# RMSNorm with a swish on one core: every load and store of x on one queue, in one fixed order

## The chip, the core and the metric

The kernel runs on one core of a Trainium2 chip. The core has engines that work side by side: VectorE (DVE in the profile), ScalarE (ACT), GpSimd (POOL) and SyncE (SP), which computes nothing here and only issues transfers. TensorE is not used. Data lives in HBM (called dram in the code) and is worked on in the on-chip memory SBUF, which has 128 partitions. Transfers between the two (DMAs) are carried by 16 DMA engines, which all queues share. An instruction on SyncE or ScalarE *issues* a transfer: it puts it into that engine's queue and goes on; the data moves later, and a semaphore is raised when all of it has landed. In the profile SyncE's queue is q1 and ScalarE's is q10.

The metric is the device time of one execution in microseconds, the median of several.

## What is computed

`x` is 16 x 1024 x 512 float32, that is 16384 rows of 512 numbers. Each row is divided by its root mean square, multiplied by `gamma`, and put through x * sigmoid(x):

```python
rms = np.sqrt(np.mean(x ** 2, axis=-1, keepdims=True) + eps)
x_norm = x / rms * gamma
return x_norm * (1.0 / (1.0 + np.exp(-x_norm)))
```

So 33.55 MB are read and 33.55 MB are written.

## The kernel before, in words

**Tiling.** The 16384 rows are cut into 8 groups of 2048. In a group each of the 128 partitions has 16 consecutive rows, so over all groups a partition has 128 rows of 2 KB. In this document "a row" is one such row in every partition, 128 x 2 KB = 262144 bytes. The buffer `xb` (line 65) holds 96 rows per partition and is worked on in place: loaded, normed, swished, stored. Groups 6 and 7 take the places of groups 0 and 1 (`slots`, line 29).

**Compute.** The work goes in 32 chunks of `cn` = 4 rows. For a chunk ScalarE squares two rows with a running sum (line 164) and two rows into PSUM (line 171), VectorE sums the latter (line 217), GpSimd makes the inverse root (lines 145 and 152), VectorE multiplies each row by it and by gamma (line 228), and ScalarE applies Silu (line 183), which raises the semaphore `s_swish`. On ScalarE the Silu of a chunk follows the squares of the chunk two later, in an order written out by hand (the loop at line 206). Gamma is loaded once by ScalarE's queue (line 201) and spread over the partitions on VectorE (line 241). Just ahead of it ScalarE's queue carries a transfer of 8 KB from a zeroed tile `blank` to a DRAM tensor `scratch` (line 197), which nothing reads.

**Transfers of x.** A load or a store is a tuple of group, first row in the group, and number of rows. The 12 loads (lines 30 to 32) are issued by SyncE, in the list's order; the first two go out ahead of the start barrier (line 125). The first nine cover the 96 rows of the buffer and wait for nothing. Load 9, the 16 rows of group 6, is issued when stores 0 and 1 have landed (`over` and `behind`, lines 115 to 118); load 10 (12 rows) follows at once, and load 11 (4 rows) when store 2 has landed. The 10 stores (lines 33 to 35) are issued by ScalarE, on its own queue, between its computations. Store 0 is held until load 7 (the 12 rows up to row 92) has landed, and store 3 until load 10 has landed (`hold`, line 36, used at lines 186 to 191). The wait stands in ScalarE's own order of instructions, so what follows it on ScalarE, a Silu among it, waits too:

```python
    def store(t):
        if t in hold:
            nc.scalar.wait_ge(ld[hold[t][0]], 16)
```

With this the transfers go in four stretches: 96 rows of loads, 32 rows of stores, 32 rows of loads, 96 rows of stores. At each change of direction a transfer of 4 rows of the old direction (load 8, store 2, load 11) is still under way when the first of the new one is issued. At the end SyncE waits for the stores that it has not yet waited for (line 250).

Of the kernel before, what the change touches and what calls it, by code (L numbers as in the profile page):

```python
# [9 lines left out]
def kernel(  # L10
# [7 lines left out]
    nc = tc.nc  # L18
    P = nc.NUM_PARTITIONS
    AF = mybir.ActivationFunctionType  # L20
    ALU = mybir.AluOpType
    fp32 = mybir.dt.float32

    xf = x.flatten_outer_dims()
    of = out.flatten_outer_dims()
    R, D = xf.shape

    groups = [16] * 8
    slots = [0, 16, 32, 48, 64, 80, 0, 16]
    loads = [(0, 0, 4), (0, 4, 4), (0, 8, 8)]  # L30
    loads += [(g, 0, 16) for g in range(1, 5)]
    loads += [(5, 0, 12), (5, 12, 4), (6, 0, 16), (7, 0, 12), (7, 12, 4)]
    stores = [(0, 0, 16), (1, 0, 12), (1, 12, 4)]
    stores += [(g, 0, 16) for g in range(2, 7)]
    stores += [(7, 0, 8), (7, 8, 8)]
    hold = {0: (loads.index((5, 0, 12)), 12), 3: (loads.index((7, 0, 12)), 22)}
    behind = {loads.index((6, 0, 16)): 1}
    ring = 96
    early = 2
    cn = 4  # L40
    n_sq = 2

    first = [sum(groups[:g]) for g in range(len(groups))]
    assert P * sum(groups) == R, R
    assert all(s + n <= ring for s, n in zip(slots, groups))

    chunks = []
    for i, (g, r, n) in enumerate(loads):
        for c in range(r, r + n, cn):
            chunks.append((slots[g] + c, i if c == r else None))  # L50
    K = len(chunks)
    assert K * cn * P == R

    ends = [-(-(first[g] + r + n) // cn) for g, r, n in stores]

    inv_d = 1.0 / float(D)
    eps_f = float(eps)
# [4 lines left out]
    def sbuf(name, shape, dt=fp32):  # L62
        return nc.alloc_sbuf_tensor(name, shape, dt).ap()

    xb = sbuf("xb", [P, ring, D])
    gamma4 = sbuf("gamma4", [P, D])
    gamma_sb = sbuf("gamma_sb", [P, D])
    neg_half = sbuf("neg_half", [P, cn])
    ms = sbuf("ms", [P, K, cn])
    aeps = sbuf("aeps", [P, K, cn])  # L70
    rstd = sbuf("rstd", [P, K, cn])
    sq = [nc.alloc_psum_tensor(f"sq{i}", [P, n_sq, D], fp32).ap() for i in range(2)]
    junk = [nc.alloc_psum_tensor(f"junk{i}", [P, D], fp32).ap() for i in range(2)]

    ld = [nc.alloc_semaphore(f"ld{t}") for t in range(len(loads))]
    st = [nc.alloc_semaphore(f"st{t}") for t in range(len(stores))]
    scratch = nc.dram_tensor("scratch", [P, 16], fp32, kind="Internal").ap()
    blank = sbuf("blank", [P, 16])
    s_blank = nc.alloc_semaphore("s_blank")
    s_scratch = nc.alloc_semaphore("s_scratch")  # L80
    s_gld = nc.alloc_semaphore("s_gld")
    s_zero = nc.alloc_semaphore("s_zero")
    s_half = nc.alloc_semaphore("s_half")
# [7 lines left out]
    s_swish = nc.alloc_semaphore("s_swish")  # L91

    def need(ins, sem, value):
        return ins.wait_op(sem, value, "sem-ge")

    def dram(ap, piece):
        g, r, n = piece
        rows = ap[P * first[g] : P * (first[g] + groups[g])]
        return rows.rearrange("(p n) d -> p n d", n=groups[g])[:, r : r + n, :]

    def place(piece):
        g, r, n = piece
        return slots[g] + r, slots[g] + r + n

    def buf(piece):
        a, b = place(piece)
        return xb[:, a:b, :]

    stored_by_sync = set()

    def load(i):
        a, b = place(loads[i])
        for u, piece in enumerate(stores):
            c, d = place(piece)
            over = piece[0] < loads[i][0] and c < b and a < d
            if (over or behind.get(i) == u) and u not in stored_by_sync:
                nc.sync.wait_ge(st[u], 16)
                stored_by_sync.add(u)
        return nc.sync.dma_start(  # L119
            out=buf(loads[i]), in_=dram(xf, loads[i])  # L120
        ).then_inc(ld[i], 16)

    entry = nc.main_func.blocks[0].instructions
    here = nc.cur_bb.bb.instructions
    for t in range(early):
        ins = load(t).ins
        assert here[-1] is ins or here[-1].name == ins.name
        here.pop()
        at = next(
            i for i, other in enumerate(entry)  # L130
            if other.engine == mybir.EngineType.SP
            and isinstance(other, mybir.InstDrain)
        )
        entry.insert(at, ins)
    for t in range(early, len(loads)):
        load(t)
    nc.sync.wait_ge(s_scratch, 16)

    nc.gpsimd.memset(blank, 0.0).then_inc(s_blank, 1)  # L139
    nc.gpsimd.memset(gamma4, 0.0).then_inc(s_zero, 1)  # L140
    nc.gpsimd.memset(neg_half, -0.5).then_inc(s_half, 1)  # L141
    nc.gpsimd.wait_ge(s_half, 1)
    for k in range(K):
        need(
            nc.gpsimd.tensor_scalar(  # L145
                out=aeps[:, k, :], in0=ms[:, k, :], scalar1=eps_f, scalar2=None,
# [6 lines left out]
                out=rstd[:, k, :], in0=aeps[:, k, :], in1=neg_half, op=ALU.pow  # L153
# [2 lines left out]
        ).then_inc(s_rstd, 1)  # L156

    def square(k):
        at, landing = chunks[k]
        if landing is not None:  # L160
            nc.scalar.wait_ge(ld[landing], 16)  # L161
        for j in range(n_sq, cn):
            n = k * (cn - n_sq) + j - n_sq
            acc = nc.scalar.activation(  # L164
                out=junk[n % 2], in_=xb[:, at + j, :], func=AF.Square,
                scale=inv_d**0.5, accum_out=ms[:, k, j : j + 1],
            )
            if n >= 2:
                need(acc, s_acc, n - 1)
            acc.then_inc(s_acc, 1)  # L170
        square = nc.scalar.activation(  # L171
            out=sq[k % 2], in_=xb[:, at : at + n_sq, :],
            func=AF.Square, scale=inv_d**0.5,
        )
        if k >= 2:
            need(square, s_sum, k - 1)
        square.then_inc(s_sq, 1)

    def swish(k):
        at, _ = chunks[k]  # L180
        rows = xb[:, at : at + cn, :]
        need(
            nc.scalar.activation(out=rows, in_=rows, func=AF.Silu), s_norm, k + 1  # L183
        ).then_inc(s_swish, 1)

    def after(t):
        return max((k for u, (_, k) in hold.items() if u <= t), default=0)

    def store(t):
        if t in hold:  # L190
            nc.scalar.wait_ge(ld[hold[t][0]], 16)  # L191
        need(
            nc.scalar.dma_start(out=dram(of, stores[t]), in_=buf(stores[t])),  # L193
            s_swish, ends[t],
        ).then_inc(st[t], 16)

    need(nc.scalar.dma_start(out=scratch, in_=blank), s_blank, 1).then_inc(
        s_scratch, 16
    )
    need(  # L200
        nc.scalar.dma_start(out=gamma4[0:P:32, :], in_=gamma.partition_broadcast(4)),
        s_zero, 1,
    ).then_inc(s_gld, 16)
    nc.scalar.preload_act_table_set("silu_and_others")  # L204
    stored = 0
    for k in range(K + 3):
        if k < K:
            square(k)
        while stored < len(stores) and max(ends[stored] + 2, after(stored)) <= k:
            store(stored)  # L210
            stored += 1
        if 2 <= k < K + 2:
            swish(k - 2)

    def sums(k):
# [6 lines left out]
        ).then_inc(s_sum, 1)  # L222

    def norm(k):
        at, _ = chunks[k]
        for j in range(cn):
            row = xb[:, at + j, :]
            ins = nc.vector.scalar_tensor_tensor(  # L228
                out=row, in0=row, scalar=rstd[:, k, j : j + 1], in1=gamma_sb,
                op0=ALU.mult, op1=ALU.mult,  # L230
            )
            if j == 0:
                need(ins, s_rstd, k + 1)
        ins.then_inc(s_norm, 1)

    for k in range(K + 1):
        if k < K:
            sums(k)
        if k == 0:
            need(  # L240
                nc.vector.stream_shuffle(gamma_sb, gamma4, [0] * 32), s_gld, 16  # L241
            ).then_inc(s_gamma, 1)
        if k == 1:
            nc.vector.wait_ge(s_gamma, 1)
        if k >= 1:
            norm(k - 1)
# [39 lines left out]
```

## Time and profile before

| what | value |
|---|---|
| median of 3 runs | 160.73 us (160.39 to 161.25) |
| profiled execution, first to last instruction (span) | 159.0 us |
| bytes moved in the profiled execution | 67.16 MB, mean 422 GB/s |
| ScalarE busy | 129.6 us (82%) |
| VectorE busy | 124.4 us (78%) |
| GpSimd busy | 65.4 us (41%) |

The profile gives the profiled execution no other time than its span; the median of the runs is 1.73 us above it. Times inside the profile are counted from the span's start. Busy times are summed per engine. The DMA row of a page counts how many of the 16 DMA engines were carrying a packet; a packet is put down to the stretch that it starts in, so that a short stretch can show more than all 16 engines at work, and only stretches of several microseconds are to be compared.

### The profile page before, as it was taken

The numbers are of one execution on the slowest core, as the hardware profiler recorded it, in microseconds if no ns is written. First come the engines' busy times: TensorE is split into PE (matmuls) and PEld (weight loads), VectorE is DVE, ScalarE is ACT, GpSimd is POOL, SyncE is SP. The second block draws the span as 40 slices with busy tenths as digits, with TensorE's granted clock in tenths as the row PEclk, the third lists the DMA queues.
The fourth block names the chain that finished last, engine by engine and source line by source line (L and its number), as shares of the span: only waits on it lengthen the run. The fifth ranks groups of instructions, "written<-read, shape, count | busy, mean of one in ns | idle before, by whom it ended". The sixth has DMA issues, their size and how long they took to land.

```text
span 159.0 us, 507 instructions
## 1 busy us (share of the span) xinstructions
DVE 124.4 (78%) x162; ACT 129.6 (82%) x193; POOL 65.4 (41%) x71
## 2 busy tenths in 40 slices
DVE  0129999999999990299999999999999999994000
ACT  0946999999999913999999999999999999947000
POOL 2035555555555550055555555555555555550000
DMA  7999999999999999989899999999999999999997
GB/s 262 441 489 396 420 486 412 396 470 453 389 422 433 433 400 433 503 367 470 363 410 396 455 408 416 443 495 420 396 462 447 412 404 478 437 396 453 387 441 301
DMA packets 3324, 67.16 MB, mean 422 GB/s; under 512 B 500, under 2 KB 500, under 8 KB 504
## 3 DMA queue, kind: packets, MB, share of 16 engines
q1 hardware_dynamic: 1728, 33.56, 49.8%
q10 hardware_dynamic: 1592, 33.57, 49.2%
q14 instruction: 4, 0.03, 0.0%
HBM read 33.56 MB, written 33.56 MB: 422 GB/s over the span
## 4 chain that ended last, share of the span: by engine, by line
ACT 65%; DMA 12%; issue 5%; DVE 4%; ACTq 2%; another core or an unknown queue 2%; SPq 0%
ACT xb L183 27%; ACT junk L164 22%; ACT sq L171 16%; DMA xb<-in_x_dram 12%; DVE xb L228 3%; ACTq L193 2%; DVE ms L217 1%; SPq L119 0%; ACTq L191 0%; ACTq L161 0%
## 5 line engine op out<-in xcount | busy, mean ns | idle before, releaser
L228 DVE SCALAR_TENSOR_TENSOR xb<-xb,rstd,gamma_sb 128x512 f32<-128x512 f32 x128 | 87.2, 744 | 0.0
L183 ACT ACTIVATE xb<-xb 128x2048 f32<-128x2048 f32 x32 | 60.9, 1902 | 10.4 <-issue 6.3
L217 DVE TENSOR_REDUCE ms<-sq 128x2 f32<-128x1024 f32 x32 | 39.1, 1223 | 17.7 <-ACT sq L171 14.5
L145 POOL TENSOR_SCALAR aeps<-ms 128x4 f32<-128x4 f32 x32 | 20.6, 644 | 71.9 <-DVE ms L217 71.9
L152 POOL TENSOR_TENSOR rstd<-aeps,neg_half 128x4 f32<-128x4 f32 x32 | 44.0, 1376 | 2.7
L164 ACT ACTIVATE junk<-xb 128x512 f32<-128x512 f32 x64 | 37.2, 582 | 3.2 <-DMA xb<-in_x_dram 3.2
L171 ACT ACTIVATE sq<-xb 128x1024 f32<-128x1024 f32 x32 | 32.2, 1005 | 0.0
L164 ACT ACTIVATION_READ_ACCUMULATOR junk<-xb 128x1 f32 x64 | 11.9, 187 | 0.0
L204 ACT ACT_TABLE_LOAD x1 | 1.3, 1283 | 3.6 <-issue 3.6
L241 DVE LOAD_MASK_SELECT gamma_sb<-gamma x1 | 0.0, 14 | 2.8 <-DMA gamma<-in_gamma_dram 2.8
L139 POOL MEMSET blank<- 128x16 f32 x1 | 0.1, 112 | 1.5 <-POOLq L60 1.5
L241 DVE STREAM_SHUFFLE gamma_sb<-gamma 128x512 f32<-128x512 f32 x1 | 0.7, 717 | 0.0
L140 POOL MEMSET gamma<- 128x512 f32 x1 | 0.5, 524 | 0.0
L267 POOL MEMSET const-float32-0.0<- 128x1 f32 x1 | 0.1, 98 | 0.2 <-issue 0.2
L267 POOL MEMSET const-uint8-127<- 128x1 uint8 x1 | 0.1, 102 | 0.0
L267 POOL MEMSET const-bfloat16-1.0<- 128x1 bf16 x1 | 0.1, 101 | 0.0
L141 POOL MEMSET neg_half<- 128x4 f32 x1 | 0.1, 101 | 0.0
L267 POOL MEMSET const-float32-1.0<- 128x1 f32 x1 | 0.1, 98 | 0.0
## 6 DMA issues: line engine op xcount, KB each, us to landing
out_dram<-xb ACTq DMA_DIRECT2D x6, 4096.0 KB, 19.2
xb<-in_x_dram SPq DMA_DIRECT2D x5, 4096.0 KB, 28.8
xb<-in_x_dram SPq DMA_DIRECT2D x2, 3072.0 KB, 37.0
xb<-in_x_dram SPq DMA_DIRECT2D x4, 1024.0 KB, 13.3
out_dram<-xb ACTq DMA_DIRECT2D x2, 2048.0 KB, 13.0
out_dram<-xb ACTq DMA_DIRECT2D x1, 3072.0 KB, 19.0
xb<-in_x_dram SPq DMA_DIRECT2D x1, 2048.0 KB, 10.3
out_dram<-xb ACTq DMA_DIRECT2D x1, 1024.0 KB, 19.8
```

What stands on the lines that cost most here:

```text
L140: nc.gpsimd.memset(gamma4, 0.0).then_inc(s_zero, 1)
L145: nc.gpsimd.tensor_scalar(out=aeps[:, k, :], in0=ms[:, k, :], scalar1=eps_f, scalar2=None, op0=ALU.add,),
L152: nc.gpsimd.tensor_tensor(out=rstd[:, k, :], in0=aeps[:, k, :], in1=neg_half, op=ALU.pow),
L164: acc = nc.scalar.activation(out=junk[n % 2], in_=xb[:, at + j, :], func=AF.Square, scale=inv_d**0.5, accum_out=ms[:, k, j : j + 1],)
L171: square = nc.scalar.activation(out=sq[k % 2], in_=xb[:, at : at + n_sq, :], func=AF.Square, scale=inv_d**0.5,)
L183: nc.scalar.activation(out=rows, in_=rows, func=AF.Silu), s_norm, k + 1
L193: nc.scalar.dma_start(out=dram(of, stores[t]), in_=buf(stores[t])),
L204: nc.scalar.preload_act_table_set("silu_and_others")
L217: nc.vector.tensor_reduce(out=ms[:, k, 0:n_sq], in_=sq[k % 2], op=ALU.add, axis=mybir.AxisListType.X,),
L228: ins = nc.vector.scalar_tensor_tensor(out=row, in0=row, scalar=rstd[:, k, j : j + 1], in1=gamma_sb, op0=ALU.mult, op1=ALU.mult,)
L241: nc.vector.stream_shuffle(gamma_sb, gamma4, [0] * 32), s_gld, 16
L267: nc = _bacc.Bacc("TRN2", target_bir_lowering=False, num_devices=1)
```

## The change

All loads and all stores of x are issued by SyncE, on its one queue, in one order written out as a list: loads of rows 0 to 99, stores of rows 0 to 31 in pieces of 16, 8 and 8, loads of rows 100 to 127 in pieces of 12, 12 and 4, and then the stores of rows 32 to 127. A piece is now a first row (of the 128 of a partition) and a number of rows. The buffer is a ring of 100 rows per partition: row r lies at r modulo 100. A store carries its wait for `s_swish` on the issuing instruction; a load waits for the stores whose places it overwrites. The holds, the `behind` wait, the scratch transfer and its zeroed tile are gone, and ScalarE issues gamma alone. The chunks and the computation stay as they are.

```diff
-    slots = [0, 16, 32, 48, 64, 80, 0, 16]
-    loads = [(0, 0, 4), (0, 4, 4), (0, 8, 8)]
-    loads += [(g, 0, 16) for g in range(1, 5)]
-    loads += [(5, 0, 12), (5, 12, 4), (6, 0, 16), (7, 0, 12), (7, 12, 4)]
-    stores = [(0, 0, 16), (1, 0, 12), (1, 12, 4)]
-    stores += [(g, 0, 16) for g in range(2, 7)]
-    stores += [(7, 0, 8), (7, 8, 8)]
-    hold = {0: (loads.index((5, 0, 12)), 12), 3: (loads.index((7, 0, 12)), 22)}
-    behind = {loads.index((6, 0, 16)): 1}
-    ring = 96
+    ring = 100
+    loads = [(0, 4), (4, 4), (8, 8), (16, 16), (32, 16), (48, 16), (64, 16), (80, 16)]
+    loads += [(96, 4), (100, 12), (112, 12), (124, 4)]
+    stores = [(0, 16), (16, 8), (24, 8), (32, 16), (48, 16), (64, 16), (80, 16)]
+    stores += [(96, 4), (100, 12), (112, 8), (120, 8)]
+    order = [("load", i) for i in range(loads.index((100, 12)))]
+    order += [("store", t) for t in range(3)]
+    order += [("load", i) for i in range(loads.index((100, 12)), len(loads))]
+    order += [("store", t) for t in range(3, len(stores))]
...
     def load(i):
-        a, b = place(loads[i])
-        for u, piece in enumerate(stores):
-            c, d = place(piece)
-            over = piece[0] < loads[i][0] and c < b and a < d
-            if (over or behind.get(i) == u) and u not in stored_by_sync:
+        a, n = loads[i]
+        for u, (c, m) in enumerate(stores):
+            over = c + ring < a + n and a < c + m + ring
+            if over and u not in stored_by_sync:
                 nc.sync.wait_ge(st[u], 16)
                 stored_by_sync.add(u)
...
+    def store(t):
+        need(
+            nc.sync.dma_start(out=dram(of, stores[t]), in_=buf(stores[t])),
+            s_swish, ends[t],
+        ).then_inc(st[t], 16)
...
-    for t in range(early, len(loads)):
-        load(t)
-    nc.sync.wait_ge(s_scratch, 16)
-
-    nc.gpsimd.memset(blank, 0.0).then_inc(s_blank, 1)
+    for what, t in order[early:]:
+        load(t) if what == "load" else store(t)
+
...
     def square(k):
-        at, landing = chunks[k]
-        if landing is not None:
+        at = k * cn % ring
+        for landing in landings[k]:
             nc.scalar.wait_ge(ld[landing], 16)
...
-    def store(t):
-        if t in hold:
-            nc.scalar.wait_ge(ld[hold[t][0]], 16)
-        need(
-            nc.scalar.dma_start(out=dram(of, stores[t]), in_=buf(stores[t])),
-            s_swish, ends[t],
-        ).then_inc(st[t], 16)
-
-    need(nc.scalar.dma_start(out=scratch, in_=blank), s_blank, 1).then_inc(
-        s_scratch, 16
-    )
...
-    stored = 0
-    for k in range(K + 3):
+    for k in range(K + 2):
         if k < K:
             square(k)
-        while stored < len(stores) and max(ends[stored] + 2, after(stored)) <= k:
-            store(stored)
-            stored += 1
-        if 2 <= k < K + 2:
+        if k >= 2:
             swish(k - 2)
```

More of the change, by code (lines that the diff above doesn't have):

```diff
@@ L43 @@
     first = [sum(groups[:g]) for g in range(len(groups))]
[L44 to L54, printed above, removed]
+    rows_each = sum(groups)
+    assert P * rows_each == R, R
+    assert ring % cn == 0
+    for pieces in (loads, stores):
+        assert [a for a, _ in pieces] == [
+            sum(n for _, n in pieces[:i]) for i in range(len(pieces))
+        ]
+        assert sum(n for _, n in pieces) == rows_each
+    K = rows_each // cn
+    landings, seen = [], 0
+    for k in range(K):
+        landings.append([])
+        while seen < len(loads) and loads[seen][0] < (k + 1) * cn:
+            landings[k].append(seen)
+            seen += 1
+    ends = [-(-(a + n) // cn) for a, n in stores]
     inv_d = 1.0 / float(D)
@@ L76 @@
     st = [nc.alloc_semaphore(f"st{t}") for t in range(len(stores))]
[L77 to L80, printed above, removed]
     s_gld = nc.alloc_semaphore("s_gld")
@@ L96, in dram @@
     def dram(ap, piece):
-        g, r, n = piece
+        a, n = piece
+        g = max(g for g in range(len(groups)) if first[g] <= a)
+        r = a - first[g]
+        assert r + n <= groups[g], piece
         rows = ap[P * first[g] : P * (first[g] + groups[g])]
         return rows.rearrange("(p n) d -> p n d", n=groups[g])[:, r : r + n, :]
-    def place(piece):
-        g, r, n = piece
-        return slots[g] + r, slots[g] + r + n
     def buf(piece):
-        a, b = place(piece)
-        return xb[:, a:b, :]
+        a, n = piece
+        at = a % ring
+        assert at + n <= ring, piece
+        return xb[:, at : at + n, :]
     stored_by_sync = set()
     def load(i):
-        a, b = place(loads[i])
-        for u, piece in enumerate(stores):
-            c, d = place(piece)
-            over = piece[0] < loads[i][0] and c < b and a < d
-            if (over or behind.get(i) == u) and u not in stored_by_sync:
+        a, n = loads[i]
+        for u, (c, m) in enumerate(stores):
+            over = c + ring < a + n and a < c + m + ring
+            if over and u not in stored_by_sync:
                 nc.sync.wait_ge(st[u], 16)
@@ L179, in swish @@
     def swish(k):
-        at, _ = chunks[k]
+        at = k * cn % ring
         rows = xb[:, at : at + cn, :]
@@ L184, in swish @@
         ).then_inc(s_swish, 1)
-    def after(t):
-        return max((k for u, (_, k) in hold.items() if u <= t), default=0)
-    def store(t):
-        if t in hold:
-            nc.scalar.wait_ge(ld[hold[t][0]], 16)
-        need(
-            nc.scalar.dma_start(out=dram(of, stores[t]), in_=buf(stores[t])),
-            s_swish, ends[t],
-        ).then_inc(st[t], 16)
-    need(nc.scalar.dma_start(out=scratch, in_=blank), s_blank, 1).then_inc(
-        s_scratch, 16
-    )
     need(
@@ L224, in norm @@
     def norm(k):
-        at, _ = chunks[k]
+        at = k * cn % ring
         for j in range(cn):
```

## Prediction

> **What bounds the kernel now.** I read four things in this order: the page's top, the table of stretches, the waits of SyncE's queue, and the chain that ended last. From the page:
>
> ```profile
> span 159.0 us, 507 instructions
> ...
> DVE 124.4 (78%) x162; ACT 129.6 (82%) x193; POOL 65.4 (41%) x71
> ...
> DMA  7999999999999999989899999999999999999997
> ...
> q1 hardware_dynamic: 1728, 33.56, 49.8%
> q10 hardware_dynamic: 1592, 33.57, 49.2%
> ...
> ACT 65%; DMA 12%; issue 5%; DVE 4%; ACTq 2%; another core or an unknown queue 2%; SPq 0%
> ```
>
> No computing engine is above 82%. The packets of the two queues together take 49.8 + 49.2 = 99.0% of the time of the 16 DMA engines, and only the first and the last slice of the DMA row are visibly below nine tenths. The chain that ended last speaks against this with its "ACT 65%". It follows the last store back to the Silu that released it. But that store was issued at 146.82 and its 8 rows landed only at the end of the span, some 12 us later, although 8 rows need 8 x 0.605 = 4.8 us (262144 bytes at 433 GB/s are 0.605 us a row). It stood behind stores already queued. So the transfers bound the kernel, and what matters is where the flow is below its full rate. The table of stretches gives that (stretch in us; length; busy time of DVE, ACT and POOL; the clock of an engine not used here; DMA share; GB/s):
>
> ```profile
> 12.00:56.00 44.00, 42.29 (x55) 42.18 (x65) 22.49 (x22) 1.00 1.00 431
> 104.00:144.00 40.00, 38.89 (x52) 37.90 (x56) 20.14 (x20) 1.00 1.00 433
> 56.00:64.00 8.00, 3.89 (x6) 1.73 (x2) 2.04 (x2) 1.00 1.04 440
> 96.00:104.00 8.00, 7.76 (x11) 8.00 (x13) 4.11 (x5) 1.00 1.04 445
> 76.00:84.00 8.00, 7.76 (x11) 8.00 (x13) 4.11 (x5) 1.00 1.00 392
> 76.00:86.00 10.00, 9.76 (x14) 10.00 (x18) 5.91 (x6) 1.00 1.03 412
> 77.00:85.00 8.00, 7.76 (x12) 8.00 (x13) 4.11 (x5) 1.00 1.01 397
> ```
>
> Pure loads run at 431 GB/s, pure stores at 433. The two switches from loads to stores (near 60 and 100) lie in stretches of 440 and 445: nothing is lost there. The one switch from stores to loads (near 79) lies in 392 to 412. That is the only hole between start and end. The waits of SyncE's queue say why it is there:
>
> ```profile
> SPq L117 <- DMA out_dram<-xb: 73.0, 1, 73.0
> SPq L119 <- DMA out_dram<-xb: 1.0, 1, 1.0
> ```
>
> SyncE stood until 78.4 on the landing of store 1 (that is L117) and issued load 9 at 78.49. Of the stores only the 4 rows of store 2 were then left, 4 x 0.605 = 2.4 us at most; that store landed at 80.9, which is when the second wait ended. The stores ran out while the loads were only starting.
>
> **The change part by part.** The sum is made against the span of 159.0 us. The profile has no other time for this execution; the median, 160.73, is 1.73 us above it, and I let that stand unchanged.
>
> The floor first: 256 rows (128 in, 128 out) x 0.605 = 154.9 us, so 159.0 - 154.9 = 4.1 us are not flow. The stretch from 0 to 4 moves 260 GB/s, which costs (1 - 260/433) x 4 = 1.6 us. The same two loads go out ahead of the barrier in both kernels, so this stays. The change can touch the hole at 79 and the scratch transfer; the rest is start and tail, and the last store is 8 rows in both.
>
> The switch from stores to loads, removed: deficits of the three stretches against 433 are (1 - 392/433) x 8 = 0.76, (1 - 412/433) x 10 = 0.49, and (1 - 397/433) x 8 = 0.66 us. A packet counts in the stretch it starts in, and the 2 us from 84 to 86 that the longest stretch adds show 492 GB/s, more than the flow can carry: it borrows from later. So I take 0.76, and keep 0.49 as the other end.
>
> What is at that place in the new order? Load 9 (rows 100 to 111) waits for store 0 (16 rows) alone. When that has landed, stores 1 and 2, 16 rows or 9.7 us, are still queued on the same queue, against 2.4 us before. Load 10 waits for store 1 and has 8 + 12 rows ahead of it (12.1 us), load 11 waits for store 2 and has 24 rows ahead (14.5 us), and store 3 is issued right behind it. A landing is seen about a microsecond late and an issue takes 0.33 to 0.99 us (the line of the loads), so every one is queued long before its turn. What a switch inside one queue costs is shown by no row. From below: nothing, as in the stretches with the well-covered switches near 60 and 100 (a gain below nothing is excluded, the flow being at its full rate there). From above: 0.76, the switch near 79, which is the only one in this direction. I take nothing: with 9.7 us queued ahead, it is nearest to the switches whose successor was waiting.
>
> The two switches from loads to stores: near 60 and 100 they cost nothing with two queues. With one queue the stores of rows 0 to 31 need chunks 4, 6 and 8, whose Silus end at about 30, 38 and 46 (one every 3.99 us: L183 starts at 28.13, 32.12, 36.11), and their turn comes after 100 loads, at about 1.6 + 100 x 0.605 = 62. They are queued 16 us early. Bounds again 0 and 0.76 each; I take 0.
>
> The scratch transfer, removed: ScalarE's queue takes 1.8% of the DMA engines from 4 to 8 us and 1.2% from 8 to 12, together 0.12 us, gamma included. Gain 0.12, at least 0. Gamma is issued 0.45 us earlier (2.04 for 2.49); VectorE waited 2.8 us for it, but compute is not on the path.
>
> Stores leave ScalarE: the hold for load 7 kept the Silu of the eleventh chunk back by 6.28 us ("ACT xb L183 <- issue: 6.3"). Without it the last Silu ends near 146.8 - 6.3 = 140.5 instead of 146.8. Gain nothing, since the transfers hide it, and if that cover were gone it would be at most 6.3.
>
> Stores on SyncE wait for Silus, and behind such a wait stand all later issues of SyncE; nobody else waits on SyncE. Due times, by rows ahead in the order x 0.605 + 1.6: store 3 (160 rows ahead) 98, needs chunk 12, done near 62; the 12 rows from 100 (228 ahead) 139.5, chunk 28, near 126; the next 8 (240) 147, chunk 30, near 134; the last 8 (248) 152, chunk 32, near 141. The least slack is 11 us, so 0. The 11 issues added to SyncE at below 1 us each lie in the same slack. Loads for compute: row 100 is wanted by chunk 26 near 116 and lands near 90.
>
> The ring of 100: the 4 rows more are loaded before the first switch and fewer after it; the bytes are the same. Cost 0.
>
> Sum: -0.76 - 0.12 = -0.88. Span 158.1, median 160.73 - 0.88 = 159.85.
>
> **A rule beside the row.** The row is the hole near 79 and none near 60 and 100. The Trainium skill, "DMA: Bandwidth & Descriptors", section "Issuing engines are not separate DMA queues", speaks against any effect: transfers issued by different engines run on the same 16 DMA engines, and the choice of issuer only changes issue time. By that rule alone the hole would stay and the time would be 160.73. The same page, section "Two DMAs through the same engine are not ordered", says that inside one queue descriptors start in order but are pipelined; by that the hole goes and the time is that of my sum. The trace agrees with the first in the rates (431 and 433 GB/s on either queue) and says nothing on switches inside one queue.
>
> **The rivals.** A switch could cost the same wherever it is queued: the slow reads after 79 would then come from the turn itself, not from the late issue. For it: the first loads of the kernel also start slowly (260 GB/s up to 4 us). Against it: there too, nothing was queued ahead. Only the scratch transfer is saved then: 160.73 - 0.12 = 160.6. It is also the case of a change that does nothing.
>
> The slower one: with two queues a DMA engine that has finished its last load takes up a store from the other queue while other work is still in flight, and the switches near 60 and 100 are free because of that. In one queue each engine must go through the switch in order, and may stall at all three. At a price p each, the time changes by 3p - 0.88, so it is slower by over 0.80 from p = 0.56 up. At the price of the hole, 0.76, it is +1.40, or 162.1. At the price of the kernel's start, 1.6, it is +3.9, or 164.6. For it: no row shows a switch inside a queue, and the free ones all had two. Against it: within either queue one transfer follows another at 431 to 433 GB/s, with no step where one ends.
>
> Compute as the new bound is a third: the last store would have to be released later than about 152, and its chunk is due near 141. It would take 11 us of new delay, where 6.3 are removed; I give it no chance of its own.
>
> **How the numbers follow.** 0.5%, about what a measurement of this kernel can tell from no change, is 0.80 us; 159.93 is the line. Covered switches: 0.56, time 159.85, own range 159.4 to 160.3 (the hole at 0.49 gives 160.1; the runs of before spread over 0.9 us). Its middle is only just past the line, but the smaller reading of the hole is the weaker one, so 0.42 of it is faster and 0.14 the same. The switch that keeps its price: 0.14, same. Switches that cost in one queue: 0.30, slower. Together 0.42, 0.28, 0.30. The range runs from 159.4 to 162.2: it leaves out the dearer half of the slow rival, some 0.15.
>
> **What the profile after would show.** If I am right: a stretch of 8 us around the stores-to-loads switch, now near 82, at 425 GB/s or more; the same near 62 and 98; SyncE's queue with 99% of the packets' time, ScalarE's with gamma alone; the last Silu ending near 140; a span near 158.1. If the second case holds, a stretch near 82 stays below 412. If the third, the stretches near 62 and 98 fall below 420 as well. Silus ending after 150, or a load issued after the stores ahead of it have run out, would make the working wrong in its slack and not in its switches.

## The result, and the profile after

The changed kernel is slower: 161.42 us (161.28 to 161.94, 9 runs) against 160.53 us for the kernel before, a ratio of 1.0068 (95% interval 1.0054 to 1.0082). The forecast was 159.85. The time lies inside the range given, but on the other side of the kernel before than forecast. Of the runs below, three of the five executions of the kernel with late loads took 164.8 to 165.1 us, over 1.5% more than its fastest, and are left out of its ratio.

The page of the changed kernel, in the lines that answer to those shown of before:

```profile
span 160.6 us, 503 instructions
...
DVE 124.5 (78%) x162; ACT 129.6 (81%) x193; POOL 65.4 (41%) x70
...
DMA  7999999999999999999999999999999999899993
...
q1 hardware_dynamic: 3312, 67.11, 98.1%
q14 instruction: 4, 0.03, 0.0%
q10 hardware_dynamic: 8, 0.01, 0.0%
...
ACT 63%; DMA 12%; issue 7%; DVE 4%; SPq 0%; ACTq 0%
```

One queue now carries all of x. The dip near the middle of the DMA row is gone, but the last slice falls from 7 tenths to 3: something ends late. The table of stretches of the changed kernel (columns as before) looks at the three turns:

```profile
56.00:64.00 8.00, 7.74 (x10) 8.00 (x13) 4.09 (x4) 1.00 1.01 391
76.00:84.00 8.00, 7.74 (x10) 8.00 (x14) 4.09 (x4) 1.00 1.04 444
96.00:104.00 8.00, 7.74 (x10) 8.00 (x14) 4.09 (x4) 1.00 1.03 436
104.00:144.00 40.00, 33.62 (x44) 33.62 (x46) 16.36 (x16) 1.00 1.00 432
```

The hole near 79 is gone as forecast (444 for 392 GB/s). A new one of the same size is at the first turn, from loads to stores: 391 for 440 GB/s, which is (1 - 391/433) x 8 = 0.78 us. The last turn is free. So the holes of both kernels come to the same, and that does not make it slower. They are not alike, though, by the packets' own times in the trace. In the kernel before the first 32 KB load packets behind the turn are slow: between 79 and 80 they take 1.80 us (median), from 82 on 1.21. In the changed kernel the first 32 KB store packets take 1.21 at once, and the last loads ahead of the turn are slow: their 8 KB packets take 0.31 us up to 61 and 0.51 to 0.52 from 61 to 63 (medians).

The waits of SyncE's queue show no shortage either:

```profile
SPq L127 <- ACT xb L189: 93.2, 10, 24.7
SPq L121 <- DMA out_dram<-xb: 37.5, 3, 28.5
```

SyncE waits long, but ahead of time: the last store is issued at 140.4 and lands 20.1 us later, behind what was queued. The last Silu ends at 140.4, as worked out.

What is slower is the very end. The stretch from 158 to 160, first in the kernel before, then in the changed one:

```profile
158.00:160.00 2.00, 0.00 (x0) 0.00 (x0) 0.00 (x0) 1.00 0.02 8
```

```profile
158.00:160.00 2.00, 0.00 (x0) 0.00 (x0) 0.00 (x0) 1.00 0.08 33
```

One engine of 16 is a share of 0.06, and 433/16 = 27 GB/s. After 158 the changed kernel moves 33 GB/s: little more than one engine's work. The trace also has a 4-byte completion packet for each DMA on each of the 16 engines; their times show how far the last engine is behind the median one (us from the span's start, worked out from the trace's records):

```
completed, DMA                     before: median  last     after: median  last
load of rows 48 to 63                      40.62  41.05            40.56  40.82
load of rows 64 to 79                      50.33  51.23            50.30  51.14
last load before the first turn            60.11  61.01            63.36  64.85
last load of all                           99.88 100.28            99.81 102.06
last store                                158.11 158.63           157.99 160.24
```

The median engine ends 0.12 earlier in the changed kernel, which is the size of the scratch term. The last one is 2.25 us behind instead of 0.52 (the last but one is 1.1 behind). Together: -0.12 + 2.25 - 0.52 = +1.61, which is the last completion's move (158.63 to 160.24) and the growth of the span (159.0 to 160.6). The profiled execution was timed at 161.94, the highest of the nine; their spans go from 160.0 to 160.6, so the loss varies from run to run, and by the medians it is 0.89 and not 1.6.

The table also says when. Between 41 and 51 the last engine falls from 0.3 or 0.4 to 0.8 or 0.9 behind, in both kernels alike. In the changed kernel it is 1.5 behind at the end of the last load before the first turn, where the slow packets are, and 2.25 at the end of the last load of all. In the kernel before the lag goes from 0.8 at the end of store 2 to 0.4 at the end of load 9, over the hole near 79.

### The profile page after: what moved, and what is told of

It is laid out like the page before. It is cut to its first block, busy times and chain, and to the rows that moved or that the text cites. A ratio compares the mean times of both kernels' runs of the same rounds, so it can differ in the third digit from the quotient of the medians.

```text
span 160.6 us, 503 instructions
## 1 busy us (share of the span) xinstructions
DVE 124.5 (78%) x162; ACT 129.6 (81%) x193; POOL 65.4 (41%) x70
## 4 chain that ended last, share of the span: by engine, by line
ACT 63%; DMA 12%; issue 7%; DVE 4%; SPq 0%; ACTq 0%
ACT xb L189 25%; ACT junk L170 22%; ACT sq L177 16%; DMA xb<-in_x_dram 12%; DVE xb L216 3%; DVE ms L205 1%; SPq L121 0%; ACTq L167 0%
```

## The experiments

The runs shared runs of the kernel before, whose median was 160.3 to 160.5; ratios are to those.

**What makes the hole at the first turn?** Four kernels.

The scratch transfer put back on ScalarE's queue:

```diff
...
+    need(nc.scalar.dma_start(out=scratch, in_=blank), s_blank, 1).then_inc(
+        s_scratch, 16
+    )
     need(
         nc.scalar.dma_start(out=gamma4[0:P:32, :], in_=gamma.partition_broadcast(4)),
...
```

> The changed kernel with the scratch transfer of 8 KB back at the head of ScalarE's queue, SyncE's final wait for it included. The new hole (stretch 56 to 64 us at 391 GB/s in the changed kernel, 440 before) and 161.42 us against 160.53 are to be explained. Theory 'cold store': the first store of a run is slow, and the scratch transfer had paid for that at the start; then the stretch 56 to 64 is back at 425 or more and the time is near 160.6. Rival 'switch in one queue': loads followed by stores in one queue are slow wherever they stand; then the stretch stays near 391 and the time is 161.4 to 161.5.

Measured: 161.75 us (ratio 1.0095, 1.008 to 1.011), the stretch at 391. The time is some 0.3 above what the rival expected, but the theory of a cold store falls: the rate of the stretch did not come back.

The scratch transfer taken out of the kernel before:

```diff
...
-    nc.sync.wait_ge(s_scratch, 16)
...
-    need(nc.scalar.dma_start(out=scratch, in_=blank), s_blank, 1).then_inc(
-        s_scratch, 16
-    )
...
```

> The kernel before without the scratch transfer, its zeroed tile and the wait for it; nothing else moves. 'Cold store': the stretch 56 to 64 falls from 440 to about 391 and the time rises by about 0.9, to 161.4. 'Switch in one queue': the stretch stays near 440 and the time is that of the kernel before or 0.1 less, 160.4 to 160.5.

Measured: 160.42 us (1.0014, 0.9997 to 1.0031), the stretch at 440. No effect that can be told from none. My 0.12 for it is not visible in the time.

The first three stores issued from ScalarE again:

```diff
-    order += [("store", t) for t in range(3)]
...
+    def store(t, eng=nc.sync):
...
             square(k)
+        if k == 12:
+            nc.scalar.wait_ge(ld[loads.index((80, 16))], 16)
+            for t in range(3):
+                store(t, nc.scalar)
         if k >= 2:
             swish(k - 2)
```

> The changed kernel with its first three stores (rows 0 to 31) issued from ScalarE's queue, held there until the load of rows 80 to 95 has landed, as the kernel before does it; all else from SyncE, no scratch transfer. 'Switch in one queue': the stretch 56 to 64 is back at 425 or more and the time near 160.5. 'Cold store': nothing has warmed this queue either, the stretch stays near 391 and the time near 161.4.

Measured: 160.88 us (1.0044, 1.0025 to 1.0063), between the two expectations. The stretches near the first and the second turn:

```profile
56.00:64.00 8.00, 4.00 (x6) 0.24 (x1) 2.04 (x2) 1.00 1.06 451
...
76.00:84.00 8.00, 7.76 (x11) 8.00 (x13) 4.11 (x5) 1.00 1.01 369
```

The hole at the first turn is gone and one at the second is there, larger: here loads start on one queue while 16 rows of stores are still on the other, and both move side by side at 369 GB/s with the engines all busy (share 1.01). So crossing queues frees the first turn. That it is the two kinds in flight on two queues that make the second one dear is not shown: no other run has them.

A ring of 96, so that the first stretch ends with packets of 32 KB:

```diff
-    ring = 100
+    ring = 96
...
-    loads += [(96, 4), (100, 12), (112, 12), (124, 4)]
+    loads += [(96, 16), (112, 12), (124, 4)]
```

> The changed kernel with a ring of 96 rows: the first stretch of loads ends with the 16 rows from 80, in packets of 32 KB, not with the 4 rows from 96 in packets of 8 KB; the second is 16, 12 and 4 rows. 'Cold store' and 'switch in one queue' both expect the hole to stay, moved 2.4 us earlier, with about 392 GB/s in the stretch 54 to 62 and a time of 161.3 to 161.5. If it is the small packets ahead of the switch that are slow, the stretch is at 425 or more and the time near 160.6.

Measured: 162.19 us (1.011, 1.0092 to 1.0129), the stretch 54 to 62 at 360. The hole is larger and the time longer than expected (392; 161.3 to 161.5). The small packets are not the cause: here too the last loads ahead of the turn are the slow ones, with 32 KB packets of 1.49 to 2.03 us (medians from 57 to 60) for 1.21.

**Does every turn cost?** One more turn on the one queue:

```diff
-    order = [("load", i) for i in range(loads.index((100, 12)))]
-    order += [("store", t) for t in range(3)]
+    order = [("load", i) for i in range(loads.index((64, 16)))]
+    order += [("store", 0)]
+    order += [("load", i) for i in range(loads.index((64, 16)), loads.index((100, 12)))]
+    order += [("store", t) for t in range(1, 3)]
```

> The changed kernel with one more change of direction on its queue: after the loads of rows 0 to 63 comes the store of rows 0 to 15, then the loads of rows 64 to 99, then the stores of rows 16 to 31, and the rest as before. Loads now turn to stores near 40, 72 and 98 us, where they did near 62 and 98. The scratch transfer on ScalarE's queue did not help the changed kernel and its loss did not hurt the kernel before, so the first store of the core is not what is slow. Theory 'every switch': each turn from loads to stores in one queue costs what the first did, 0.9 us; then the stretches 36 to 44 and 68 to 76 both read about 391 GB/s and the time is 162.2 or more. Rival 'first of the queue': only the first store on a queue is slow; then 36 to 44 reads 391, 68 to 76 reads 425 or more, and the time stays at 161.4 to 161.6.

Measured: 161.74 us (1.0082, 1.0068 to 1.0095). The stretches at the first two turns from loads to stores:

```profile
36.00:44.00 8.00, 7.74 (x10) 8.00 (x14) 4.09 (x4) 1.00 0.94 337
...
68.00:76.00 8.00, 7.76 (x11) 8.00 (x13) 4.09 (x4) 1.00 0.99 408
```

The hole went to the first turn, at more than twice its size (1.77 us by the rate, where 391 would be 0.78), and the second, the same as the first turn of the changed kernel but for its place, lost 0.46. That is nearer to "the first of the queue", though 408 is short of the 425 expected. But the next kernel speaks against a simple form of that, a scratch transfer on SyncE's own queue:

```diff
...
+    need(nc.sync.dma_start(out=scratch, in_=blank), s_blank, 1).then_inc(
+        s_scratch, 16
+    )
     for what, t in order[early:]:
         load(t) if what == "load" else store(t)
...
```

> The changed kernel with the scratch transfer of 8 KB on SyncE's queue, behind the first two loads. 'First of the queue': this pays for the first store at the start, the stretch 56 to 64 is at 425 or more and the time near 160.6. 'Every switch': the stretch stays near 391 and the time is 161.4 to 161.7.

Measured: 162.0 us (1.0102, 1.0088 to 1.0115), the stretch 56 to 64 at 390. A store of 8 KB does not pay for it. The time is 0.3 above what "every switch" expected.

A kernel meant to have no hole, with the queues crossed at each turn from loads to stores:

```diff
-    order += [("store", t) for t in range(3)]
-    order += [("load", i) for i in range(loads.index((100, 12)), len(loads))]
...
+        if (what, t) == ("store", 3):
+            nc.sync.wait_ge(ld[loads.index((112, 12))], 16)
...
+        if k == 12:
+            nc.scalar.wait_ge(ld[loads.index((80, 16))], 16)
+            for t in range(3):
+                store(t, nc.scalar)
+        if k in (15, 17, 18):
+            load({15: 9, 17: 10, 18: 11}[k], nc.scalar)
```

> A kernel meant to have no hole: loads of rows 0 to 99 on SyncE's queue, the stores of rows 0 to 31 and behind them the loads of rows 100 to 127 on ScalarE's, the stores of rows 32 to 127 on SyncE's again, each first store held as in the kernel before until only 4 rows of loads are left. Every turn from loads to stores crosses queues, the turn from stores to loads stays inside one. No scratch transfer, ring of 100 rows. 'Switch in one queue' expects the stretches 56 to 64, 78 to 86 and 94 to 102 all at 425 or more; with holes adding up the time is near 159.7 (160.5 less 0.76), with a laggard setting the end near 160.2.

Measured: 160.69 us (1.0016, 1.0007 to 1.0025). The first turn is free and the hole is at the second, inside one queue and with its loads queued in time (the first was issued at 73.7, the stores ended at 83):

```profile
56.00:64.00 8.00, 3.87 (x5) 0.10 (x1) 2.04 (x2) 1.00 1.07 455
...
78.00:86.00 8.00, 7.76 (x11) 8.00 (x13) 4.11 (x5) 1.00 1.00 385
94.00:102.00 8.00, 7.76 (x11) 8.00 (x13) 4.11 (x5) 1.00 1.01 431
```

So a turn from stores to loads inside one queue is not free as such. The slow packets are again the last ones ahead of the turn: 16 KB packets of the stores take 1.21 us between 81 and 82, and 0.62 before. In all of these kernels at least one hole stands somewhere; what places it stays open.

**Does a hole cost the end?** The first loads of the second stretch issued late:

```diff
-    stores = [(0, 16), (16, 8), (24, 8), (32, 16), (48, 16), (64, 16), (80, 16)]
+    stores = [(0, 16), (16, 12), (28, 4), (32, 16), (48, 16), (64, 16), (80, 16)]
...
+            late = a == 100 and u == 1
+            if (over or late) and u not in stored_by_sync:
```

> The changed kernel with the first loads after the first stores issued late, as in the kernel before: the stores of rows 0 to 31 go as 16, 12 and 4 rows, and the load of rows 100 to 111 waits for the first two, so that only 4 rows are left ahead of it. The hole of about 0.75 us that the kernel before has at that place comes back (a stretch of 8 us near 80 at 390 to 400 GB/s). Theory 'holes add up': the time rises by 0.75, to 162.2. Rival 'laggard': in the changed kernel one of the 16 DMA engines ends 2.2 us after most of the others and sets the end, and a hole lets it catch up; then the time rises by less than 0.3, to 161.2 to 161.7, and the flow at the end stops more sharply (the stretch 156 to 161 above 164 GB/s).

Measured: ratio 1.0135 (1.0115 to 1.0155), from two executions of 162.22 and 162.88 us. The first turn keeps its hole (386 GB/s from 56 to 64). The expected hole came larger than in the kernel before and brought another at the third turn:

```profile
78.00:86.00 8.00, 7.76 (x11) 8.00 (x13) 4.11 (x5) 1.00 0.89 340
94.00:102.00 8.00, 7.76 (x11) 8.00 (x13) 4.09 (x4) 1.00 0.96 364
```

As to time neither theory had it: the two holes together are about 3 us, (1 - 340/433) x 8 and (1 - 364/433) x 8, and by the ratios (1.0135 against 1.0068) the time rose by 1.1. As to the engines the laggard theory had it: the last one was 1.6 us behind the median before the hole and 0.45 after it, 0.47 at the end.

**The transfers alone.** All computation was left out of both kernels. One queue, and two queues:

```diff
...
-        need(
-            nc.sync.dma_start(out=dram(of, stores[t]), in_=buf(stores[t])),
-            s_swish, ends[t],
-        ).then_inc(st[t], 16)
+        for i, (a, n) in enumerate(loads):
+            if a < sum(stores[t]) and stores[t][0] < a + n:
+                nc.sync.wait_ge(ld[i], 16)
+        nc.sync.dma_start(out=dram(of, stores[t]), in_=buf(stores[t])).then_inc(
+            st[t], 16
+        )
...
```

> The transfers of the changed kernel alone: all computation and gamma are left out, a store waits for the loads of its own rows, and the order on SyncE's queue is the same; what is stored is x. With no computation there is next to no program to fetch on the way (packets on the instruction queue near 40 and 44 us fell on a DMA engine that later ended last). Theory 'laggard': what the changed kernel lost is one DMA engine that falls behind and is put further back at each turn from loads to stores; without the fetches it does not fall behind, and this is within 0.3 of the two-queue transfers alone. Rival 'one queue costs the same for all engines': this is 0.9 slower than the two-queue transfers alone, as the kernels were.

> The transfers of the kernel before alone, left out in the same way: loads on SyncE's queue, stores on ScalarE's with the same holds, no scratch transfer. Reference for the other. Both theories expect a hole of 0.75 us near 79 and a span within 1 us of the full kernel's.

Measured: 160.16 us with one queue (0.9979, 0.9967 to 0.9991) and 160.07 with two (0.9976, 0.9958 to 0.9994): the same. The one-queue transfers at the first turn and at the end:

```profile
56.00:64.00 8.00, 0.00 (x0) 1.00 1.03 393
...
158.00:160.00 2.00, 0.00 (x0) 1.00 0.00 0
```

The two-queue transfers at the three turns:

```profile
56.00:64.00 8.00, 0.00 (x0) 1.00 1.04 442
76.00:84.00 8.00, 0.00 (x0) 1.00 1.06 420
96.00:104.00 8.00, 0.00 (x0) 1.00 0.98 417
```

The hole of the one-queue order is still there (393), so it is not made by computation, and it makes no difference to the time between the orders. The late engine is gone: nothing starts after 158, and the last engine is 0.6 us behind the median. The two-queue transfers do not have the hole of 0.75 us that was expected near 79, but smaller ones at the second and the third turn (0.24 and 0.30 us). Nor did the engines come together near 79 here: the lag of the last one was 0.10 us at the end of store 2 and 1.44 at the end of load 9. It was 0.9 after the third turn and 0.7 at the end. (This profile is of an execution of 160.65 us, 0.6 above the median.)

Then one DMA engine was held up by an extra packet, in either order:

```diff
+    nc.scalar.wait_ge(ld[5], 16)
+    nc.scalar.dma_start(out=pad, in_=xb[0:1, 32:48, :]).then_inc(s_pad, 16)
```

> The one-queue transfers alone, with one packet of 32 KB put on a single DMA engine near 41 us: a store of 16 rows of one partition to a tensor that nothing reads, on ScalarE's queue. It holds that engine up by 1.2 us, 0.08 on the mean of 16. 'Laggard': the engine keeps the 1.2 and loses up to 0.8 more at each of the two turns from loads to stores, so the time is 1.2 to 2.8 above the one-queue transfers alone. Rival: a delay of one engine does not matter, 0 to 0.2 above.

> The two-queue transfers alone with the same packet on a single DMA engine near 41 us. 'Laggard': the hole near 79 lets the engine catch up, so the time is 0 to 0.5 above the two-queue transfers alone. If nothing lets it catch up it is 1.2 above.

Measured: 162.68 us with one queue, 2.5 above; 161.07 with two queues, 1.0 above. The one-queue order keeps the delay to the end, as this stretch shows (22 GB/s, less than one engine's 27):

```profile
158.00:161.00 3.00, 0.00 (x0) 1.00 0.05 22
```

By the completion packets the held engine was 1.8 us behind the median at 52, 2.05 at 62, 2.9 with the last load before the first turn, and 2.9 at the end. In the two-queue order it was 1.7 behind at 52, 1.0 after the turn near 60 and 0.5 after the one near 80. But catching up was not free: there the time rose by 1.0, where I had allowed 0.5. The stretch 56 to 64 fell to 379, the one from 76 to 84 to 376. Its holds wait for all 16 engines, so a late one can delay what the other 15 do next; that this is all of the 1.0 is not shown.

**What holds the engine up in the full kernel?** The transfers alone, with program to fetch:

```diff
...
+    nc.gpsimd.wait_ge(ld[4], 16)
+    for i in range(300):
+        nc.gpsimd.memset(tiny[:, i : i + 1], 0.0)
```

> The one-queue transfers alone (160.16 us), with 300 small memsets on GpSimd from the landing of rows 32 to 47, near 31 us, on: no data of x is touched, but program has to be fetched while the loads run. Theory 'fetch makes the laggard': packets on the instruction queue appear between 31 and 61, one DMA engine ends about 1 to 2 us after the others, and the time is 160.7 to 161.7. Rival 'it is the computing engines' use of the memory': nothing of that kind is here, the time stays within 0.3 of 160.16.

> The two-queue transfers alone (160.07 us) with the same 300 memsets. 'Fetch makes the laggard': the engine is held up as much, but the waits of the two-queue order let it catch up; 0 to 0.5 above 160.07, so 160.1 to 160.6, and less than the one-queue transfers with the memsets. Rival: unchanged, and equal to the one-queue transfers with the memsets.

Measured: 162.28 us with one queue (2.1 above the transfers alone, more than expected), 160.88 with two (0.8 above, also more). The DMA queues of the one-queue run from 31 to 61 us, and its end:

```profile
q1 hardware_dynamic: 473, 12.58, 98.0%
q14 instruction: 2, 0.02, 0.1%
```

```profile
158.00:160.00 2.00, 0.00 (x0) 1.00 0.06 25
```

Two packets of 8 KB, 16 KB in 67 MB, are on the instruction queue, and one engine is late at the end (2.2 us behind the median). No computing engine touches x in this kernel. The packets also show whom the fetch hits. An engine's 32 KB load packets follow each other without a gap, 1.21 us each. So one engine's packets can be told from another's. Both fetched packets stand in gaps of one and the same engine, which resumes 0.31 us later with a packet of 1.56 us each time. In the changed kernel the packets fetched at 40.4 and 44.1 us hit two engines in this way (1.58 and 1.88 us), and these two are the last at 61.

With two queues the profile is of the longest of twelve executions, 162.06 us against the median of 160.88. In it the last engine is 1.4 us behind at 61, 0.9 at the end of store 2, 1.6 at the end of load 9, and 0.7 at the end, and the stretch 76 to 84 is at 364 GB/s. So the late engine did not catch up near 79 here, and what this execution lost is lost by all engines: the median one ends at 159.7 (158.3 in the transfers alone).

The other way round, the full kernels with a shorter program:

```diff
...
-        for j in range(n_sq, cn):
-            n = k * (cn - n_sq) + j - n_sq
-            acc = nc.scalar.activation(
...
-        for j in range(cn):
+        for j in range(1):
             row = xb[:, at + j, :]
```

> The full changed kernel (161.42 us) with a shorter program: the squares with running sums, and the normalization of rows 1 to 3 of every chunk, are left out, so ScalarE and VectorE have 2 instructions a chunk instead of 5; the Silus, the transfers and their waits stay. 'Fetch makes the laggard': the packets on the instruction queue at 40 and 44 us come later or not at all, and the time falls to 160.2 to 160.8. Rival: Silus still read and write the whole buffer, the time stays within 0.3 of 161.42.

> The full kernel before (160.53 us) with the same work left out. Both theories expect 160.0 to 160.6: what the engine loses there it makes up at the hole near 79. With 'fetch makes the laggard' the gap to the changed kernel with the shorter program is below 0.4, without it 0.9.

Measured: 160.73 us with one queue (1.0012, 0.9998 to 1.0026) and 160.76 with two (1.0021, 1.0006 to 1.0036). The gap is gone. The two kernels' queues from 36 to 56 us, the changed kernel first, the same with the shorter program second:

```profile
q1 hardware_dynamic: 287, 8.36, 97.3%
q14 instruction: 2, 0.02, 0.2%
```

```profile
q1 hardware_dynamic: 288, 8.39, 97.4%
```

The instruction queue has nothing in that stretch any more (its three packets come at 60.8, 69.6 and 78.0), and the last engine ends 1.0 us behind the median, not 2.25. This run alone could also be put down to the lighter computation; the one before, with no computation on x, cannot. The two figures of the order before, 160.53 and 160.76, differ little, as expected if the delay is made up there.

## Why the prediction was wrong

Point by point, by its own steps:

- **The transfers bound the kernel.** Right: with no computation at all either order takes 160.1 to 160.2.
- **The hole near 79 goes.** Right for this kernel (444 GB/s). The reason given, that loads queued in time make the turn free, is not enough: in the kernel with crossed queues they were queued in time behind the stores and the hole was there (385).
- **The two turns from loads to stores cost nothing in one queue.** Failed at the first turn: 0.78 us where I took 0 and gave 0 to 0.76 as bounds. I took the free turns of the trace as nearest because work was queued ahead; what they had was two queues. The third turn is free by the rate. With this alone the sum would have been -0.10, no measurable change.
- **"The rest is start and tail", unchanged.** This is the step that failed and that decides the sign: I treated the 16 engines as one flow, with one rate and one end. The last DMA is done when its slowest engine is done, and that one moved from 0.52 to 2.25 us behind the median.
- **Compute and SyncE's order.** Right: Silus end at 140.4, and no turn ran out of issued work. (Stores 1 and 2 of the kernel before were seen 0.4 to 0.5 us after their last completion packet, not a microsecond; it changes nothing.)
- **Scratch, 0.12.** The median engine's end moved by 0.12, but taking the transfer out of the kernel before showed no gain, so that agreement may be chance.
- **The slower rival** had the right sign with the wrong mechanism: it had a price at all three turns for all engines. One turn cost, another turn gave it back, and the time was lost by one engine. I also set the sum against a median 1.73 us above the span; the profiled execution after was timed at 1.34 above its own.

The cause as the runs show it: fetching program puts packets on single DMA engines while the loads run, and an engine that is hit falls behind. In one queue with work always queued ahead nothing stops the others for it, and it falls back further around the turns (0.65 and 0.8 us in the profile after, 0.8 and nothing in the run with the held engine). In the order before, load 9 starts only when all engines have finished store 1 and little is queued behind; in that profile the late engine caught up there (0.8 to 0.4). That such a wait can do it, and not the second queue alone, is shown by the kernel with late loads on one queue (1.55 to 0.45). At the end the last engine is 1.6 to 2.4 us behind in the kernels that compute everything, have one queue and no late loads, and 0.4 to 0.7 in every profile with two queues.

That fetch delays the engine, and that this costs time in one queue, is shown by adding program and by taking it away. Two things are not shown. One is why a late engine loses more at a turn. The other is where the two-queue order makes up the delay: the hole that I counted as waste was paying for it in the profile before, but in the two-queue transfers alone and in those with program the lag rose over that place and fell at other turns.

The Trainium skill, "DMA: Bandwidth & Descriptors", section "Two DMAs through the same engine are not ordered", has a sentence that I read past: "Nothing at all orders DMAs across the 16 engines." The completion packets agree with it: within one queue the last engine drifts to 2.25 us behind the median. What the section "Issuing engines are not separate DMA queues" says, that the choice of issuer saves issue time only, agrees with the transfers alone (160.16 against 160.07 us); the full kernels differ (161.42 against 160.53), but in their waits as well as in the issuer.

Still open is what places the one hole. It was at the second turn in the kernel before, the one with three stores moved and the crossed one, at the first in all that had only one queue there, and with late loads all three turns had one. In the packets some of these holes are slow last packets ahead of the turn and others slow first packets behind it, so they need not have one cause. A theory of "every turn", of "the first store", or of "late issue" each fails on one of these runs. No version tried that computes the result beats the kernel before.

## What to carry to other kernels

Where transfers set the time, read the last microseconds by DMA engine: a share near 0.06 of the 16 engines is one late engine, and it sets the end of the kernel. A wait on a completed transfer that seems to cost a gap may be what brings the engines back together, so price its removal by the slowest engine and not by the mean rate.

## What was not expected of the hardware

Two packets of 8 KB on the instruction queue, in transfers of 67 MB, cost 2.1 us in one order and 0.8 in the other. One packet of 32 KB on one engine cost 2.5 and 1.0. In one kernel loads and stores in flight side by side on two queues ran at 369 GB/s over 8 us, where either alone runs at 431 to 433. In the changed kernel the first turn slowed the last packets ahead of it (8 KB in 0.52 us for 0.31) and not the first ones behind it.
